# First norm of a two-layer decoder trunk: squares of x as the weights of one-column matmuls, and an inverse root in nine VectorE instructions

## The chip, the core and the metric

The kernel runs on one core of a Trainium2 chip. A core has TensorE (PE, with its weight loads listed apart as PEld), VectorE (DVE), ScalarE (ACT), GpSimdE (POOL) and SyncE (SP, which issues most DMAs). The metric is the device time of one execution in microseconds. All data are float32; most large products split their operands into a high and a low part and sum three products of parts.

## The reference

x has 512 tokens of 1024 channels, and c is one conditioning vector. Two layers follow each other, each with a token mixer (layer 0 a state-space mixer called S5, layer 1 an attention called FoX) and a gated feed-forward network with a short convolution (FFN). Ahead of each of the four sub-layers stands a norm by token, whose result is scaled and shifted by values computed from c; a last norm ends the kernel. This is the part that the change touches:

```python
def rmsnorm(x, g):
    x32 = x.astype(jnp.float32)
    y = x32 * lax.rsqrt(jnp.mean(x32 * x32, axis=-1, keepdims=True) + EPS)
    return (y * g.astype(jnp.float32)).astype(x.dtype)

def adaln_params(c, w, b):
    mod = jax.nn.silu(c) @ w + b
    shift, scale, gate = jnp.split(mod, 3, axis=-1)
    return shift[:, None, :], scale[:, None, :], gate[:, None, :]

def modulate(x, g, shift, scale):
    return rmsnorm(x, g) * (1.0 + scale) + shift

for i in range(DEPTH):                                  # DEPTH = 2
    shift, scale, gate = adaln_params(c, ada_w[i, 0], ada_b[i, 0])
    hn = modulate(h, norm_g[i, 0], shift, scale)
    m = s5_mixer(hn, ...) if i % 2 == 0 else fox_mixer(hn, ...)
    h = h + gate * m
    ...                                                 # the same with conv_ffn
return rmsnorm(h, final_g)
```

## The kernel before

The residual `h` lies in on-chip memory as eight tiles of 128 channels by 512 tokens (KT = 8, S = 512); a block of 128 tokens is one of NB = 4. So a sum over channels is a sum over partitions and over the eight tiles, and it is done by matmuls.

The work runs in stages, one after another: a prologue (the first norm and the start of S5), the S5 stage, FFN 0, FoX, FFN 1 and the last norm. In the prologue the order on PE, ACT, DVE and SP is the order in which the code is written (`manual_schedule`). Elsewhere a scheduler orders the instructions of each engine from the dependences and from costs that it assumes, so an edit in one place can move instructions of its neighbourhood. Each engine runs its own queue in order and waits for other engines by semaphores. A tile from a pool with n buffers can be written only when the tile n places earlier has been read for the last time.

The first norm, in `s5`, goes like this. SP issues four loads of `x`, then the loads of the first modulation's weights `ada_w`, 512 KB each, into `raw`, `w_hi` and `w_lo` buffers. ACT squares one tile of h after another into `nm_t` (L1113), a pool of two buffers. PE multiplies each square by a 128x128 matrix of ones (L1114): the sums over channels come out on all 128 partitions, with the 512 tokens along the row. ACT copies the sums (L1116), and PE turns the four blocks of 128 tokens around with transposes (L1119), so that each partition holds its own token's sum; column 0 of each block is the input of the inverse root.

The inverse root (`inv_root`, L391 to L401) starts from an integer trick and corrects twice, in eleven DVE instructions on a few columns, each of which needs the one before. In the prologue they are interleaved with the 25 instructions of `s5_turns` on `s_turn`, which need nothing of the norm. Behind them on DVE stands more parameter work of S5 (L701 to L881), then `ga` (L167), then the normed x, `a_x` (L1130).

On PE, behind the norm, stand 16 matmuls of the first modulation (`ada_pe`, L205, with the vector c as weights of 32 columns and `ada_w` as the moving operand, four of them side by side in the array), then `rms_rows` (L410), which spreads the inverse roots along rows, then the columns of the modulation (`ada_columns`, L157 and L162), whose result feeds `ga`. `a_x` needs `ga` and L410; the first product of S5 (L1144) needs `a_x`, and between its matmuls stand those of the second modulation (L205 again).

The later norms use `rms_stats` (L380): DVE has added up the squares of seven tiles (`ssq`), and this sum and the eighth square are the weights of matmuls whose moving operand is the column of ones `self.one`. They work on halves of 256 tokens, so nb is 2. Then come `inv_root`, `rms_rows`, and for each tile `nm_h` (L430, DVE), `a_hi` (L433, ACT) and `a_lo` (L434, DVE). The last norm (`norm_out`) scales the second half by the root in L469 and sends it out.

Of the kernel before, what the change touches and what calls it, by code (L numbers as in the profile page):

```python
# [8 lines left out]
F32 = mybir.dt.float32  # L9
F32R = mybir.dt.float32r  # L10
I32 = mybir.dt.int32
AF = mybir.ActivationFunctionType
ALU = mybir.AluOpType
# [4 lines left out]
P = 128  # L18
D = 1024
KT = D // P  # L20
S = 512
NB = S // P
# [36 lines left out]
def fill(pool, n):  # L59

    pool.tile([P, n // 4], F32, name="fill", bufs=1)
# [12 lines left out]
class Trunk:  # L74
# [311 lines left out]
    def inv_root(self, ps, nb, log=None):  # L386
        v, r, t, y = (self.small.tile([P, nb], I32 if n == "r" else F32, name=f"rs_{n}") for n in "vrty")
        e = self.nc.vector
        f = r.bitcast(F32)
        steps = (  # L390
            lambda: e.tensor_scalar(v, ps, 1.0 / D, EPS, op0=ALU.mult, op1=ALU.add),  # L391
            lambda: e.tensor_scalar(r, v.bitcast(I32), -0.5, float(0x5F3759DF), op0=ALU.mult, op1=ALU.add),
            lambda: e.tensor_tensor(t, f, f, ALU.mult),
            lambda: e.tensor_tensor(t, t, v, ALU.mult),
            lambda: e.scalar_tensor_tensor(t, t, -1.25 / 0.375, t, op0=ALU.add, op1=ALU.mult),
            lambda: e.tensor_scalar(t, t, 0.375, 1.875, op0=ALU.mult, op1=ALU.add),
            lambda: e.tensor_tensor(y, f, t, ALU.mult),
            lambda: e.tensor_tensor(t, y, y, ALU.mult),
            lambda: e.tensor_tensor(t, t, v, ALU.mult),
            lambda: e.tensor_scalar(t, t, -0.5, 1.5, op0=ALU.mult, op1=ALU.add),  # L400
            lambda: e.tensor_tensor(y, y, t, ALU.mult),  # L401
        )
        in_turn(steps) if log is None else log.extend(steps)
        return y
# [268 lines left out]
def in_turn(*logs):  # L673

    order = sorted(((n + 0.5) / len(l), i, n) for i, l in enumerate(logs) for n in range(len(l)))
    for _, i, n in order:
        logs[i][n]()
# [104 lines left out]
class S5(Trunk):  # L782
# [297 lines left out]
    def s5(self, i, nxt):  # L1080
        nc, tc = self.nc, self.tc
# [4 lines left out]
        with ExitStack() as stack:  # L1086
            spool = lambda name, st: st.enter_context(tc.tile_pool(name=name, bufs=1, reuse_waits="tile"))
            keep = spool("s5p", stack)
            self.first = self.load_pack("first", FIRST, keep)
            nc.scalar.activation(self.sc, self.first["c"], AF.Silu)  # L1090
            ones = keep.tile([P, P], F32, name="s5_ones")
            nc.vector.memset(ones, 1.0)
            self.s5q = spool("s5q", stack)
            with ExitStack() as start:
                tp = spool("s5t", start)
# [10 lines left out]
                with tc.manual_schedule(engines={ENG.PE, ENG.Activation, ENG.DVE, ENG.SP}):  # L1106
                    self.load_x(self.act)
                    self.load_rest()
                    self.s5_planes(keep)
                    ps = self.mm.tile([P, S], F32, name="mmp")  # L1110
                    for k in range(KT):
                        sq = self.tmp.tile([P, S], F32, name="nm_t")
                        nc.scalar.activation(sq, self.h[:, k, :], AF.Square)  # L1113
                        nc.tensor.matmul(ps, ones, sq, start=(k == 0), stop=(k == KT - 1))  # L1114
                    rows = self.tmp.tile([P, S], F32, name="nm_t")
                    nc.scalar.activation(rows, ps, AF.Copy)  # L1116
                    stats = self.aux.tile([P, NB, P], F32, name="aux")
                    for b in range(NB):
                        nc.tensor.transpose(stats[:, b], rows[:, b * P:(b + 1) * P], self.ident)  # L1119
                    params = self.s5_params(keep, tp, self.first["s5_prm"], stats[:, :, 0])  # L1120
                    y = next(params)
                    scale = self.ada_pe(i, (1,), late=True)
                    for _ in range(KT // 2):
# [11 lines left out]
                    ps = self.mm.tile([P, S], F32, name="mmp")  # L1135
# [71 lines left out]
            ps = self.aux.tile([KT, P], F32, name="aux")  # L1207
            nc.tensor.transpose(ps, self.sc, self.ident)
            rows = self.tmp.tile([KT, P], F32, name="nm_h", bufs=4)
# [61 lines left out]
        with tc.tile_pool(name="s5b", bufs=1, reuse_waits="tile") as pool:  # L1271
# [15 lines left out]
            after, y = nxt  # L1287
# [358 lines left out]
```

## Time and profile before

| | |
|---|---|
| time, median of 3 runs | 1217.13 us (1215.23 to 1223.22) |
| the profiled execution | 1217.02 us, its span from first to last instruction 1215.2 us |
| TensorE busy | 1180.3 us (97%), weight loads 1015.4 us (84%) |
| VectorE busy | 1007.6 us (83%) |
| ScalarE busy | 609.8 us (50%) |
| GpSimdE busy | 83.9 us (7%) |
| mean granted TensorE clock | 0.995 |
| moved by DMA | 183.81 MB, 151 GB/s on average |

All times in rows are microseconds from the first instruction. A row of the timeline holds start, duration, engine, line, operation, tiles as out<-in, shape, count, and in brackets the engine's idle time before it with what ended it. A row of the chain of waits holds start, duration, and what ran there. A row of the table by stretch holds the stretch, its length, then for PE, PEld, DVE, ACT and POOL the busy time and number of instructions, then the granted clock of PE (1.00 is full), the busy share of the DMA engines and the GB/s. A matmul of float32 operands appears as two records on PE, each with a weight load; most of the large products are one record. Ends of matmuls are modelled, so start-to-start distances tell more than durations.

### The profile page before, as it was taken

The numbers are of one execution on the slowest core, as the hardware profiler recorded it, in microseconds if no ns is written. First come the engines' busy times: TensorE is split into PE (matmuls) and PEld (weight loads), VectorE is DVE, ScalarE is ACT, GpSimd is POOL, SyncE is SP. The second block draws the span as 40 slices with busy tenths as digits, with TensorE's granted clock in tenths as the row PEclk, the third lists the DMA queues.
The fourth block names the chain that finished last, engine by engine and source line by source line (L and its number), as shares of the span: only waits on it lengthen the run. The fifth ranks groups of instructions, "written<-read, shape, count | busy, mean of one in ns | idle before, by whom it ended". The sixth has DMA issues, their size and how long they took to land.

```text
span 1215.2 us, 20334 instructions
## 1 busy us (share of the span) xinstructions
PE 1180.3 (97%) x7793; PEld 1015.4 (84%) x7793; DVE 1007.6 (83%) x1872; ACT 609.8 (50%) x1156; POOL 83.9 (7%) x145
## 2 busy tenths in 40 slices
PE   7999999999999999999999999999999999999997
PEld 2566688898989899889899777878989999999987
DVE  7999977789899988898687578875899887888965
ACT  3644555336445454455443565654466554555543
POOL 0000000100000000000000333430000000000000
PEclk9999999999999999999999999999999999999999
DMA  9778786622455544553445543432213332333331
GB/s 348 243 250 261 233 294 220 210 77 70 136 179 164 189 155 148 169 168 106 126 153 180 172 153 130 148 108 88 89 53 113 112 119 90 103 104 109 109 100 70
DMA packets 74512, 183.81 MB, mean 151 GB/s; under 512 B 23231, under 2 KB 25631, under 8 KB 73391
## 3 DMA queue, kind: packets, MB, share of 16 engines
q1 hardware_dynamic: 68367, 161.02, 40.5%
q0 software_dynamic: 5760, 20.97, 5.4%
q8 instruction: 61, 1.00, 0.3%
q10 hardware_dynamic: 288, 0.52, 0.1%
q14 instruction: 36, 0.29, 0.1%
HBM read 175.57 MB, written 6.92 MB: 150 GB/s over the span
## 4 chain that ended last, share of the span: by engine, by line
PE 56%; issue 26%; DVE 8%; DMA 5%; ACT 2%; POOL 2%; SPq 0%; POOLq 0%; DVEq 0%; ACTq 0%
PE mmp L294 24%; PE mmp L550 11%; PE aux L550 4%; PE mmp L1366 3%; PE mmp L1174 2%; DVE w_lo L278 2%; PE mmp L1203 2%; POOL ada_raw L233 1%; PE aux L1505 1%; DMA ada_raw<-in_ada_t 1%; PE aux L1065 1%; PE mmp L1114 1%; PE aux L1057 1%; PE aux L978 1%; DMA yt<-s_yd 1%
## 5 line engine op out<-in xcount | busy, mean ns | idle before, releaser
L278 DVE TENSOR_TENSOR w_lo<-raw,w_hi 128x1024 fp32r<-128x1024 f32 (+4 forms) x173 | 183.3, 1064 | 37.6 <-ACT w_hi L277 31.8
L277 ACT ACTIVATE w_hi<-raw 128x1024 fp32r<-128x1024 f32 (+4 forms) x173 | 154.8, 904 | 105.4 <-PE mmp L294 48.6
L294 PE MATMUL mmp<-ghi,w_hi 128*128 128x512 f32 (+1 forms) x392 | 145.5, 371 | 0.0
L294 PE MATMUL mmp<-ghi,w_lo 128*128 128x512 f32 (+1 forms) x392 | 144.7, 369 | 0.7 <-DVE w_lo L278 0.6
L294 PE MATMUL mmp<-glo,w_hi 128*128 128x512 f32 (+1 forms) x392 | 145.1, 370 | 0.0
L294 PE MATMUL mmp<-a_hi,w_hi 128*128 128x512 f32 (+1 forms) x376 | 138.4, 371 | 1.5 <-ACT a_hi L433 1.5
L294 PE MATMUL mmp<-a_hi,w_lo 128*128 128x512 f32 (+1 forms) x376 | 136.2, 363 | 0.2 <-DVE w_lo L278 0.2
L294 PE MATMUL mmp<-a_lo,w_hi 128*128 128x512 f32 (+1 forms) x376 | 135.7, 362 | 0.0
L550 PE MATMUL mmp<-w_hi 128*128 128x256 f32 x396 | 109.7, 277 | 2.7 <-ACT nm_h L557 2.3
L550 PE MATMUL mmp<-w_hi,w_lo 128*128 128x256 f32 x396 | 109.5, 277 | 0.7 <-DVE w_lo L278 0.7
L550 PE MATMUL mmp<-w_lo,w_hi 128*128 128x256 f32 x396 | 109.4, 276 | 0.0
L557 ACT ACTIVATE nm_h<-mmp 128x256 f32<-128x256 f32 x99 | 37.2, 381 | 107.3 <-PE mmp L550 107.3
L278 DVE TENSOR_TENSOR w_lo<-sums,w_hi 128x1024 fp32r<-128x1024 f32 x74 | 90.0, 1219 | 0.0
L277 ACT ACTIVATE w_hi<-sums 128x1024 fp32r<-128x1024 f32 x74 | 77.0, 1055 | 23.7 <-DVE sums L518 21.7
L294 PEld LDWEIGHTS mmp<-ghi,w_lo 128*128 128x128 f32 x392 | 74.7, 190 | 13.8 <-DVE w_lo L278 1.5
L294 PEld LDWEIGHTS mmp<-ghi,w_hi 128*128 128x128 f32 x392 | 74.7, 191 | 11.5 <-ACT w_hi L277 0.2
L294 PEld LDWEIGHTS mmp<-glo,w_hi 128*128 128x128 f32 x392 | 74.8, 191 | 11.1
L294 PEld LDWEIGHTS mmp<-a_hi,w_hi 128*128 128x128 f32 x376 | 70.2, 188 | 13.8 <-issue 2.6
L294 PEld LDWEIGHTS mmp<-a_hi,w_lo 128*128 128x128 f32 x376 | 70.6, 188 | 12.2 <-DVE w_lo L278 1.2
L294 PEld LDWEIGHTS mmp<-a_lo,w_hi 128*128 128x128 f32 x376 | 70.7, 188 | 9.7
L362 DVE SCALAR_TENSOR_TENSOR h<-mmp,par,h 128x512 f32<-128x512 f32 (+1 forms) x100 | 68.0, 681 | 12.1 <-PE mmp L294 11.9
L550 PEld LDWEIGHTS mmp<-w_hi 128*128 128x128 f32 x396 | 74.3, 188 | 3.2 <-ACT nm_h L557 2.5
(319 smaller groups left out, 3077.7 us busy)
## 6 DMA issues: line engine op xcount, KB each, us to landing
raw<-in_w_up SPq DMA_DIRECT2D x88, 512.0 KB, 3.3
raw<-in_ada_w SPq DMA_DIRECT2D x40, 512.0 KB, 5.6
ada_raw<-in_ada_t POOLq DMA_DIRECT2D x40, 512.0 KB, 3.9
nf<-nfd SPq DMA_DIRECT2D x8, 1152.0 KB, 6.5
raw<-in_fox_qk SPq DMA_DIRECT2D x16, 512.0 KB, 3.7
raw<-in_w_down SPq DMA_DIRECT2D x24, 320.0 KB, 3.1
rawd<-in_w_down SPq DMA_DIRECT2D x24, 256.0 KB, 3.3
raw<-in_w_down SPq DMA_DIRECT2D x16, 384.0 KB, 3.5
```

The source lines that it names most:

```text
L233: (nc.gpsimd if late else nc.sync).dma_start(ws[n], src)
L277: nc.scalar.activation(hi, src, AF.Copy)
L278: return nc.vector.tensor_tensor(lo, src, hi.bitcast(F32), ALU.subtract)
L294: self.last_mm = self.nc.tensor.matmul(o, wt, xt[:, cols], start=(k == 0 and n == 0), stop=(k == nk - 1 and n == 2),)
L362: add = self.nc.vector.scalar_tensor_tensor(self.h[:, m, cols], ps, self.par[i][:, 16 + m:17 + m], self.h[:, m, cols], op0=ALU.mult, op1=A ...
L550: self.last_mm = nc.tensor.matmul(o, wt[:, k], xt[:, k], start=(first and k == 0 and n == 0), stop=(k == H - 1 and n == 2), skip_group_che ...
L557: a = nc.scalar.activation(t, o, AF.Copy)
L978: nc.tensor.matmul(ps[:, :, cols], x[:, q, r].rearrange("p c j -> p (c j)"), both[:, :, planes, q, :], start=(r == 0), stop=(r == 1), skip ...
L1057: nc.tensor.matmul(yp[g2][:, k, :], t[:, g].rearrange("p c i -> p (c i)"), u[:, g, :], start=(k == 0), stop=False, skip_group_check=True,)
L1174: nc.tensor.matmul(ps, w[m][:, k, :], x[:, k], start=(k == 0), stop=(k == KT - 1))
L1203: nc.tensor.matmul(gps[m], wt, xt[:, k], start=(k == 0 and part == 0 and xt is yhi), stop=(k == KT - 1 and part == 1))
L1366: self.last_mm = nc.tensor.matmul(ps[q, b][:, :n], xt[:, k, tb], wt, start=(k == 0 and i == 0), stop=(k == KT - 1 and i == 2),)
```

## The change

Two edits. In the prologue the matrix of ones, the copy and the transposes go. Each block of 128 tokens of a square becomes the weights of a matmul whose moving operand is the column of ones, and the result, one number per token on that token's partition, is accumulated over the eight tiles. That is 4 matmuls for each of the eight squares, 32 in all. `fill(keep, 512)` keeps the room that the ones took, so that the other tiles stay where they were. In `inv_root`, used by all norms, a scale that was applied in an instruction of its own is carried into later constants: nine instructions in place of eleven.

```diff
         f = r.bitcast(F32)
+        a = 0.375
         steps = (
             lambda: e.tensor_scalar(v, ps, 1.0 / D, EPS, op0=ALU.mult, op1=ALU.add),
             lambda: e.tensor_scalar(r, v.bitcast(I32), -0.5, float(0x5F3759DF), op0=ALU.mult, op1=ALU.add),
             lambda: e.tensor_tensor(t, f, f, ALU.mult),
             lambda: e.tensor_tensor(t, t, v, ALU.mult),
-            lambda: e.scalar_tensor_tensor(t, t, -1.25 / 0.375, t, op0=ALU.add, op1=ALU.mult),
-            lambda: e.tensor_scalar(t, t, 0.375, 1.875, op0=ALU.mult, op1=ALU.add),
-            lambda: e.tensor_tensor(y, f, t, ALU.mult),
+            lambda: e.scalar_tensor_tensor(t, t, -1.25 / a, t, op0=ALU.add, op1=ALU.mult),
+            lambda: e.scalar_tensor_tensor(y, t, 1.875 / a, f, op0=ALU.add, op1=ALU.mult),
             lambda: e.tensor_tensor(t, y, y, ALU.mult),
-            lambda: e.tensor_tensor(t, t, v, ALU.mult),
-            lambda: e.tensor_scalar(t, t, -0.5, 1.5, op0=ALU.mult, op1=ALU.add),
-            lambda: e.tensor_tensor(y, y, t, ALU.mult),
+            lambda: e.scalar_tensor_tensor(t, t, -0.5 * a ** 3, v, op0=ALU.mult, op1=ALU.mult),
+            lambda: e.scalar_tensor_tensor(y, t, 1.5 * a, y, op0=ALU.add, op1=ALU.mult),
         )
...
-            ones = keep.tile([P, P], F32, name="s5_ones")
-            nc.vector.memset(ones, 1.0)
+            fill(keep, 512)
...
-                    ps = self.mm.tile([P, S], F32, name="mmp")
+                    stats = self.aux.tile([P, NB], F32, name="aux")
                     for k in range(KT):
                         sq = self.tmp.tile([P, S], F32, name="nm_t")
                         nc.scalar.activation(sq, self.h[:, k, :], AF.Square)
-                        nc.tensor.matmul(ps, ones, sq, start=(k == 0), stop=(k == KT - 1))
-                    rows = self.tmp.tile([P, S], F32, name="nm_t")
-                    nc.scalar.activation(rows, ps, AF.Copy)
-                    stats = self.aux.tile([P, NB, P], F32, name="aux")
-                    for b in range(NB):
-                        nc.tensor.transpose(stats[:, b], rows[:, b * P:(b + 1) * P], self.ident)
-                    params = self.s5_params(keep, tp, self.first["s5_prm"], stats[:, :, 0])
+                        for b in range(NB):
+                            nc.tensor.matmul(
+                                stats[:, b:b + 1], sq[:, b * P:(b + 1) * P], self.one,
+                                start=(k == 0 and b == 0), stop=(k == KT - 1), skip_group_check=True,
+                            )
+                    params = self.s5_params(keep, tp, self.first["s5_prm"], stats)
```

What stands first in PE's queue shows the first edit. Before (line numbers of the old file; `s_ones` is the matrix of ones, `rest` holds the identity):

```order
L1114 MATMUL mmp<-nm_t,s_ones 128x512 x8
L1119 MATMUL aux<-rest,nm_t 128x128 x4
L205 MATMUL mmp<-raw,s_sc_202 32x512 x16
L410 MATMUL aux<-rest,rs_y 128x128 x4
L157 MATMUL aux<-rest 128x8
```

And of the change (its lines count three fewer from here on; `one` is the column of ones):

```order
L1113 MATMUL aux<-one,nm_t 128x1 x32
L205 MATMUL mmp<-raw,s_sc_218 32x512 x16
L409 MATMUL aux<-rest,rs_y 128x128 x4
L157 MATMUL aux<-rest 128x8
L162 MATMUL aux<-sel,ada_rows 128x2 x4
```

The two groups at the head became one of 32, and what follows stands as before. The chain of the inverse root stands on DVE in the prologue, after the parameters of S5. Its end before:

```order
L399 TENSOR_TENSOR rs_t<-rs_t,rs_v 128x4
L908 SCALAR_TENSOR_TENSOR s_turn<-s_turn 128x32
L909 TENSOR_SCALAR s_turn<-s_turn 128x32
L907 SCALAR_TENSOR_TENSOR s_turn<-s_turn 128x32
L400 TENSOR_SCALAR rs_t<-rs_t 128x4
L908 SCALAR_TENSOR_TENSOR s_turn<-s_turn 128x32
L909 TENSOR_SCALAR s_turn<-s_turn 128x32
L401 TENSOR_TENSOR rs_y<-rs_y,rs_t 128x4
L913 TENSOR_SCALAR s_turn<-s_turn 128x6x32
```

And of the change:

```order
L399 SCALAR_TENSOR_TENSOR rs_t<-rs_t,rs_v 128x4
L906 SCALAR_TENSOR_TENSOR s_turn<-s_turn 128x32
L907 SCALAR_TENSOR_TENSOR s_turn<-s_turn 128x32
L908 TENSOR_SCALAR s_turn<-s_turn 128x32
L400 SCALAR_TENSOR_TENSOR rs_y<-rs_t,rs_y 128x4
L912 TENSOR_SCALAR s_turn<-s_turn 128x6x32
```

The root still ends just ahead of the last `s_turn` row, and two of its rows are gone. The last rows of DVE's queue are the root of the last norm's second half. Before:

```order
L391 TENSOR_SCALAR rs_v<-aux 128x2
L392 TENSOR_SCALAR rs_r<-rs_v 128x2
L393 TENSOR_TENSOR rs_t<-rs_r 128x2
L394 TENSOR_TENSOR rs_t<-rs_t,rs_v 128x2
L395 SCALAR_TENSOR_TENSOR rs_t<-rs_t 128x2
L396 TENSOR_SCALAR rs_t<-rs_t 128x2
L397 TENSOR_TENSOR rs_y<-rs_r,rs_t 128x2
L398 TENSOR_TENSOR rs_t<-rs_y 128x2
L399 TENSOR_TENSOR rs_t<-rs_t,rs_v 128x2
L400 TENSOR_SCALAR rs_t<-rs_t 128x2
L401 TENSOR_TENSOR rs_y<-rs_y,rs_t 128x2
L469 TENSOR_SCALAR o_tok<-aux,rs_y 128x512 x2
```

And of the change:

```order
L392 TENSOR_SCALAR rs_v<-aux 128x2
L393 TENSOR_SCALAR rs_r<-rs_v 128x2
L394 TENSOR_TENSOR rs_t<-rs_r 128x2
L395 TENSOR_TENSOR rs_t<-rs_t,rs_v 128x2
L396 SCALAR_TENSOR_TENSOR rs_t<-rs_t 128x2
L397 SCALAR_TENSOR_TENSOR rs_y<-rs_t,rs_r 128x2
L398 TENSOR_TENSOR rs_t<-rs_y 128x2
L399 SCALAR_TENSOR_TENSOR rs_t<-rs_t,rs_v 128x2
L400 SCALAR_TENSOR_TENSOR rs_y<-rs_t,rs_y 128x2
L468 TENSOR_SCALAR o_tok<-aux,rs_y 128x512 x2
```

Here nothing stands between the rows, and each needs the one before. At the other norms and at the start of both FFN stages the scheduler also exchanges neighbouring rows, on PE, DVE and ACT; GpSimd's and SP's queues are the same as before.

## The prediction

> **What bounds the kernel now.** I read the engine shares first, then the stages in a table by stretch, then the first 27 us instruction by instruction, since the larger edit stands there.
>
> ```profile
> PE 1180.3 (97%) x7793; PEld 1015.4 (84%) x7793; DVE 1007.6 (83%) x1872; ACT 609.8 (50%) x1156; POOL 83.9 (7%) x145
> ...
> 0.00:27.40 27.40, 18.45 (x78) 7.53 (x78) 20.39 (x145) 9.34 (x17) 2.66 (x22) 1.00 0.90 341
> 27.40:200.00 172.60, 171.29 (x1215) 115.01 (x1216) 154.45 (x239) 93.95 (x251) 1.28 (x2) 1.00 0.80 259
> ```
>
> TensorE (PE) is busy 97% of the span, and after 27.4 us it is nearly gapless (171.29 of 172.60 us). What delays that stream at its start delays the end. So the prologue is worth its full length, up to the first matmul on the normed x (L1144). These are its rows, from the timeline and the chain of waits:
>
> ```profile
> 5.54 1.15 ACT L1113 ACTIVATE nm_t<-h 128x512 f32<-128x512 f32 x2 [1.08 <-DMA h<-in_x]
> 8.33 0.63 ACT L1113 ACTIVATE nm_t<-h 128x512 f32<-128x512 f32 x1 [1.64 <-PE mmp L1114]
> 6.22 10.38 PE mmp L1114 x16
> 16.63 0.60 ACT L1116 ACTIVATE nm_t<-mmp 128x512 f32<-128x512 f32 x1 [1.22 <-PE mmp L1114]
> 17.28 0.65 PE aux L1119 x4
> 17.97 0.16 DVE L391 TENSOR_SCALAR rs_v<-aux 128x4 f32<-128x4 f32 x1 [3.12 <-PE aux L1119]
> 21.07 0.25 DVE L913 TENSOR_SCALAR s_turn<-s_turn 128x192 f32<-128x192 f32 x1
> 17.86 3.80 PE L205 MATMUL mmp<-raw,s_sc 128*32 128x512 f32 x32
> 21.60 1.16 PE L410 MATMUL aux<-rest,rs_y 128*128 128x128 f32 x8
> 22.73 1.03 PE L162 MATMUL aux<-sel,ada_rows 128*128 128x2 f32 x8
> 23.70 0.62 PE L205 MATMUL mmp<-raw,s_sc 128*32 128x512 f32 x2
> 26.44 0.16 DVE L167 SCALAR_TENSOR_TENSOR ga<-aux,rest 128x8 f32<-128x8 f32 x1
> 27.43 1.12 PE L1144 MATMUL mmp<-a_x,raw 128*128 128x512 f32 x2 [2.07 <-DVE a_x L1130]
> ```
>
> The squares on ScalarE (ACT) wait for PE, which needs 10.38 us for eight products with ones. A copy and four transposes follow. VectorE (DVE) stood idle 3.12 us before `rs_v`, then worked without a pause to `ga` at 26.44. The PE branch had its last word for `ga` at about 23.7 (L162), so DVE's queue set the start of L1144, with 2.7 us to spare on PE.
>
> The eight products did not all cost the same:
>
> ```profile
> 6.00:12.00 6.00, 5.78 (x7) 2.42 (x8) 5.62 (x44) 2.20 (x5) 0.00 (x0) 1.00 1.02 401
> 12.00:16.60 4.60, 4.59 (x10) 1.27 (x8) 2.72 (x23) 2.27 (x4) 0.00 (x0) 1.00 1.03 418
> ```
>
> Each f32 matmul is two records. Seven records touch the first 6 us and ten the next 4.6: about 0.85 us each, then about 0.43 to 0.5. The clock column says 1.00 there, but the durations say that PE began at half speed and doubled near 12 us. This doubling is the point on which I rest the forecast.
>
> **The change, part by part.**
>
> *Norm on PE (term A).* Gone are eight 128x512 products, the copy (L1116), four transposes (L1119) and a memset. New are 32 instructions with a 128x128 block of squares as weights and one moving column: 64 records, each with a full weight load. The kernel already has this shape, in the later norms (L380), once at half clock and once at full. First the table by stretch around the half-clock place, then the timeline:
>
> ```profile
> 599.34:602.76 3.42, 1.46 (x13) 1.26 (x12) 1.97 (x5) 1.17 (x3) 0.00 (x0) 1.00 0.00 0
> 602.76:606.17 3.41, 3.26 (x16) 3.26 (x16) 0.49 (x2) 2.68 (x4) 0.00 (x0) 0.50 0.01 2
> 606.17:609.58 3.41, 3.41 (x17) 3.41 (x18) 2.74 (x9) 0.42 (x1) 0.00 (x0) 0.50 0.08 11
> 609.58:613.00 3.42, 3.42 (x32) 3.42 (x32) 3.12 (x11) 0.48 (x2) 0.00 (x0) 1.00 0.84 274
> ...
> 602.91 1.01 PE L380 MATMUL aux<-one,ssq 128*128 128x1 f32 x4 [2.11 <-DVE ssq L356]
> 603.79 0.56 PE L294 MATMUL mmp<-ghi,w_hi 128*128 128x256 f32 x1
> 605.85 0.85 PE L380 MATMUL aux<-one,nm_t 128*128 128x1 f32 x4
> 606.56 0.56 PE L294 MATMUL mmp<-ghi,w_hi 128*128 128x256 f32 x1
> ...
> 1196.23 0.61 PE L380 MATMUL aux<-one,ssq 128*128 128x1 f32 x4
> 1196.70 0.36 PE L294 MATMUL mmp<-ghi,w_hi 128*128 128x256 f32 x1
> 39.42 1.95 PE L1155 MATMUL aux<-par,raw 128*128 128x1 f32 x16 [0.27 <-ACT par L170]
> 41.23 0.27 PE L1208 MATMUL aux<-rest,sc 128*8 128x128 f32 x1
> ```
>
> At half clock four records take 0.88 us (602.91 to 603.79) or 0.71 (605.85 to 606.56, the first weights loaded behind a wide matmul): 0.22 or 0.18 each. At full clock they take 0.47 / 4 = 0.12, and L1155's sixteen, 1.81 / 16 = 0.11. So a square costs 8 x 0.22 = 1.76 us at half clock and 0.94 at full, against about 1.7 and 0.9 for the wide product now. **The new form is no cheaper than the old one at the same clock.** What it saves for certain is the copy and the transposes, 16.60 to 17.93 = 1.33 us.
>
> Which clock will it have? In the stretch from 602.76 PE is busy 3.26 of 3.41 us, yet the clock stays at 0.50. Taking off the one-column records (0.88 and 0.32 us) leaves 2.06 us of wide streaming, 60%. The next stretch has 3.41 - 0.39 = 3.02 us of it, 88%, and the clock is full after it. I read this as: only streamed columns count, and the release wants more than 60% and at most 88% of a stretch of 3.41 us. The new norm streams one column per record, so I take it to stay at half clock throughout: 64 x 0.22 = 14.1, end at 6.22 + 14.1 = 20.3 (17.6 at 0.18), where today the statistics are ready at 17.93. ACT needs only some 0.6 us per square (5.54 to 6.69 for two) and isn't the limit.
>
> The Trainium skill, "TensorE: Matmul & The Clock Gate", section on the HAM clock gate, says that the array starts at 1.2 GHz and goes to 2.4 after about 3.4 us of sustained activity; the halving agrees with the rows above (0.85 to 0.43), but it doesn't say whether weight loads count as activity. By its rule taken plainly the release would come as it does now, near 12 us, and the sum would be that of the first rival.
>
> *What follows in the prologue.* DVE starts `rs_v` at 20.3 in place of 17.97: +2.3. The chain of inverse root and `s_turn`, 34 instructions from 17.97 to 21.07, is 0.09 each, so two fewer give -0.2: DVE is ready for `ga` at 26.44 + 2.1 = 28.6. PE runs L205 next (32 records, 17.86 to 21.60, 3.7 us at full clock). These stream 512 columns each, so I let them release the clock after one and a half stretches, 5.1 us: that does 2.55 us' worth, the other 1.15 follow, end at 26.6. L410 to L162 take 21.60 to 23.76 = 2.2, so `ga` can go at 28.8. **A = +2.3**; from -0.5 (0.18 per record, DVE then first) to +3.5 (L205 at half clock to the end: 20.3 + 7.4 + 2.2 = 29.9).
>
> The weight transfers move with it: raw buffers are freed by L205, so SP's next loads go later. In the table by stretch this hole is seen:
>
> ```profile
> 18.00:19.00 1.00, 1.00 (x12) 0.28 (x11) 1.00 (x12) 0.00 (x0) 0.00 (x0) 1.00 0.96 393
> 19.00:20.00 1.00, 1.00 (x12) 0.26 (x8) 1.00 (x13) 0.00 (x0) 0.00 (x0) 1.00 0.33 107
> 20.00:21.00 1.00, 1.00 (x14) 0.38 (x8) 1.00 (x13) 0.00 (x0) 0.00 (x0) 1.00 0.68 123
> ```
>
> The eight loads of the first modulation fill the queue to about 19.5. The hole ends when L205 has freed its first buffers; L205 starts 2.4 us later and its first quarter takes 0.9 us more at half clock, so the hole grows by 3.3. What is behind it is needed when L1144 starts, which is 2.3 us later itself. I add nothing; the upper end is the difference, +1.0.
>
> *The nine-instruction root in the later norms (term B).* The waits of PE that end on this chain:
>
> ```profile
> PE mmp L294 <- ACT a_hi L433: 1.5, 2, 0.8
> PE aux L410 <- DVE rs_y L401: 0.5, 2, 0.3
> ```
>
> Two steps of 0.20 us (next fence) are gone from each half. The two waits of 0.25 at L410 vanish (-0.5). Of the two of 0.76 at L433 I count 0.25 each, since DVE interleaves other work there. **B = -1.0**, from 0 to -2.0 (all of both rows).
>
> *The last norm (term C).* The kernel's end hangs on the second half's root, in the chain of waits:
>
> ```profile
> 1206.82 0.17 DVE rs_v L391
> ...
> 1208.80 0.17 DVE rs_y L401
> ...
> 1209.07 0.75 DVE o_tok L469
> ```
>
> Ten steps in 1.98 us; nothing runs beside them, so two fewer are **C = -0.4**.
>
> *Rows that only change places (term D).* The order also shifts neighbours in the norms and at the start of each FFN, where DVE is nearly full:
>
> ```profile
> L278 DVE TENSOR_TENSOR w_lo<-raw,w_hi 128x1024 fp32r<-128x1024 f32 (+4 forms) x173 | 183.3, 1064 | 37.6 <-ACT w_hi L277 31.8
> ...
> 262.00:300.00 38.00, 36.47 (x52) 1.00 0.21 70
> ```
>
> I value it at 0. From below it could close a 0.76 us gap of PE twice (-1.5), from above make PE wait for one more DVE operation of 1.06 us (the mean of L278) twice (+2.1).
>
> **The sum** against the profiled execution's own 1217.02 us (span 1215.2; 0.1 below the median, so no correction): +2.3 - 1.0 - 0.4 = +0.9, that is **1217.9 us**.
>
> **The rivals.** *(1) The clock is released as today.* If weight loads count, 6.0 us at 0.22 make 27 records to 12.25, and the other 37 x 0.12 = 4.4 end at 16.6. `rs_v` comes 1.3 earlier, with the shorter chain -1.5, and PE's 23.7 stays below the new 24.9. 1217.0 - 1.5 - 1.4 = 1214.1. For it: the page's plain wording, and a stretch at 95% busy might simply have missed a higher bar. Against: 602.76 to 606.17. Chance 0.25.
>
> *(2) It does all that its words say.* If a record costs 0.12 whatever the clock, the norm ends at 6.22 + 7.7 = 13.9, below DVE's own 14.85 (17.97 less its idle 3.12). `ga` then waits for L162 at 23.75, since the loads still fill the queue to about 19.5 and the last of L205 waits for them: -2.7. 1217.0 - 2.7 - 1.4 = 1212.9. The same page, section on LDWEIGHTS, gives columns / 1.2 ns for a load (107 ns for 128), without naming a clock; the trace agrees at full clock (0.11 to 0.12) and differs at half (0.22), and the measurement decides. Chance 0.10.
>
> *(3) Slower.* L205 uses 32 of 128 array columns per matmul. If the monitor weighs that, the clock stays half through L205, L410 and L162: 20.3 + 7.4 + 4.4 = 32.1 for `ga`, +5.7, and L1144 with its L205 neighbours spends another stretch or two of 3.41 us at half clock, which puts off +1.7 to 3.4. Together +8.2, 1217.0 + 8.2 - 1.4 = 1223.8. It decides if L205 alone doesn't lift the clock before L410. Four L205 groups run side by side, which speaks against it. Chance 0.12.
>
> **How the numbers follow.** The forecast has 0.53. A half-clock stretch like that at 602.76 costs 6.83 / 2 = 3.4 us and depends on where a gap falls, so single runs scatter (1215.2 to 1223.2 before); the range takes that in with the bounds of A to D and reaches over rivals 1 and 2 and to rival 3: 1212 to 1223.5. A difference under 1% (12 us) is what a measurement of this kernel can't tell from no change, and all cases lie inside it: within 1% 0.95, faster 0.02, slower 0.03 (rival 3 with another half-clock stretch).
>
> **What the new profile would show.** For the forecast: 64 one-column records on PE from 6.2 to about 20, squares on ACT that start about 1.7 us apart to the last, `rs_v` after 18.5, a first full-clock stretch that begins only in L205, `ga` past 27.5. Rival 1 shows the squares' spacing halving near 12 us and `rs_v` near 16.6; rival 2 squares 0.6 to 1.0 us apart and DVE without idle before `rs_v`; rival 3 L1144 records of 0.85 us. For B and C: no wait of L410 on `rs_y`, and eight steps of 0.20 before `o_tok`. The forecast is wrong if records of one column cost under 0.15 at half clock, or if the stream after 27 us has slack that swallows the shift.

## The result, and the profile after

| | before | changed |
|---|---|---|
| median | 1215.17 us (21 runs) | 1219.48 us (21 runs) |
| ratio, 95% interval | | 1.0025 [1.0014, 1.0035], that is +3.0 us (1.7 to 4.3) |
| the profiled execution | 1217.02 us | 1219.48 us (span 1217.6) |

The change made the kernel slightly slower. One execution of each kernel (of before and of the changed one, about 200 and 250 us slower than the rest) is left out of the ratio; of the other 20 the means lie 3.1 us apart and the medians 3.9. The forecast was 1217.9 us (range 1212 to 1223.5) and "within 1%". The size of the difference was missed: +0.9 forecast, +3.0 measured. That the time itself came closer is partly luck, since the profiled execution of before, on which the sum was made, lies 1.9 us above the median of its 21 runs.

Line numbers are three lower than before: the squares are L1111, the norm's matmuls L1113, the inverse root L392 to L400, `rms_rows` L409, `a_x` L1127, the first product of S5 L1141, the one-column sums L1152 (L1155 before, the name that the expectations below use). Every experiment shifts its lines by a few more, so rows are best matched by their tiles. First the timeline of the changed kernel's prologue:

```profile
5.37 1.15 ACT L1111 ACTIVATE nm_t<-h 128x512 f32<-128x512 f32 x2 [0.89 <-DMA h<-in_x]
6.05 13.81 PE L1113 MATMUL aux<-one,nm_t 128*128 128x1 f32 x64 [6.05 <-ACT nm_t L1111]
8.01 0.63 ACT L1111 ACTIVATE nm_t<-h 128x512 f32<-128x512 f32 x1 [1.49 <-PE aux L1113]
9.72 0.63 ACT L1111 ACTIVATE nm_t<-h 128x512 f32<-128x512 f32 x1 [1.08 <-PE aux L1113]
...
16.55 0.63 ACT L1111 ACTIVATE nm_t<-h 128x512 f32<-128x512 f32 x1 [1.09 <-PE aux L1113]
19.79 5.99 PE L205 MATMUL mmp<-raw,s_sc 128*32 128x512 f32 x32
19.90 0.16 DVE L392 TENSOR_SCALAR rs_v<-aux 128x4 f32<-128x4 f32 x1 [5.04 <-PE aux L1113]
...
28.35 0.16 DVE L167 SCALAR_TENSOR_TENSOR ga<-aux,rest 128x8 f32<-128x8 f32 x1
29.35 1.98 PE L1141 MATMUL mmp<-a_x,raw 128*128 128x512 f32 x4 [0.47 <-DVE a_x L1127]
```

ACT starts a square every 1.71 us from 8.01 to 16.55 without ever speeding up, because PE takes 13.81 us for 64 records, 0.216 each. DVE now stands idle 5.04 us before `rs_v` (3.12 before). `ga` comes 1.91 us later than before and L1141 1.92. The table by stretch shows where the clock rises:

```profile
8.87:12.29 3.42, 3.42 (x18) 3.42 (x18) 3.25 (x28) 1.26 (x2) 0.00 (x0) 1.00 1.04 419
12.29:15.70 3.41, 3.41 (x18) 3.41 (x18) 2.43 (x20) 1.26 (x2) 0.00 (x0) 1.00 1.03 418
...
23.00:24.00 1.00, 1.00 (x8) 0.19 (x4) 0.93 (x8) 0.00 (x0) 0.00 (x0) 1.00 0.61 156
24.00:25.00 1.00, 1.00 (x12) 0.31 (x8) 0.90 (x7) 0.00 (x0) 0.00 (x0) 1.00 0.98 377
```

The clock column reads 1.00 throughout and is no help before the first recorded change; the counts are. PE was busy to the last hundredth from 8.87 to 15.70, yet only 18 records touch each stretch. L205's records go from 8 to 12 per microsecond within 24 to 25, and in the trace's clock records the first full-clock stretch starts at 24.58. Before, it started at 12.25.

In the wait list of PE the two rows on the root that the prediction quotes are gone (two rows that are there are shown), and the chain of waits at the end is shorter:

```profile
PE mmp L549 <- ACT nm_h L556: 6.0, 4, 2.7
...
PE mmp L205 <- DMA raw<-in_ada_w: 0.4, 1, 0.4
```

```profile
1209.62 0.17 DVE rs_v L392
...
1211.20 0.17 DVE rs_y L400
...
1211.47 0.75 DVE o_tok L468
```

From `rs_v` to the last `rs_y` it is 1.58 us, against 1.98 before.

### The profile page after: what moved, and what is told of

It reads as the page before. It is cut to its first block, busy times and chain, and to the rows that moved or that the text cites. A ratio compares the mean times of both kernels' runs of the same rounds, so it can differ in the third digit from the quotient of the medians.

```text
span 1217.6 us, 20405 instructions
## 1 busy us (share of the span) xinstructions
PE 1185.9 (97%) x7837; PEld 1026.0 (84%) x7837; DVE 1006.6 (83%) x1853; ACT 608.9 (50%) x1155; POOL 83.7 (7%) x145
## 5 line engine op out<-in xcount | busy, mean ns | idle before, releaser
L294 PE MATMUL mmp<-ghi,w_hi 128*128 128x512 f32 (+1 forms) x392 | 145.9, 372 | 0.0
L294 PE MATMUL mmp<-ghi,w_lo 128*128 128x512 f32 (+1 forms) x392 | 145.0, 370 | 0.8 <-DVE w_lo L278 0.6
L294 PE MATMUL mmp<-glo,w_hi 128*128 128x512 f32 (+1 forms) x392 | 145.2, 371 | 0.0
L294 PE MATMUL mmp<-a_hi,w_hi 128*128 128x512 f32 (+1 forms) x376 | 137.8, 369 | 0.0
L294 PE MATMUL mmp<-a_hi,w_lo 128*128 128x512 f32 (+1 forms) x376 | 136.0, 362 | 0.3 <-DVE w_lo L278 0.3
L294 PE MATMUL mmp<-a_lo,w_hi 128*128 128x512 f32 (+1 forms) x376 | 135.7, 362 | 0.0
L549 PE MATMUL mmp<-w_hi 128*128 128x256 f32 x396 | 110.0, 278 | 4.8 <-ACT nm_h L556 4.3
L549 PE MATMUL mmp<-w_hi,w_lo 128*128 128x256 f32 x396 | 109.5, 277 | 1.1 <-DVE w_lo L278 1.1
L549 PE MATMUL mmp<-w_lo,w_hi 128*128 128x256 f32 x396 | 109.5, 276 | 0.0
L294 PEld LDWEIGHTS mmp<-ghi,w_lo 128*128 128x128 f32 x392 | 74.8, 191 | 14.1 <-DVE w_lo L278 1.8
L294 PEld LDWEIGHTS mmp<-ghi,w_hi 128*128 128x128 f32 x392 | 74.9, 191 | 11.7 <-ACT w_hi L277 0.4
L294 PEld LDWEIGHTS mmp<-glo,w_hi 128*128 128x128 f32 x392 | 74.9, 191 | 11.0
L294 PEld LDWEIGHTS mmp<-a_hi,w_lo 128*128 128x128 f32 x376 | 70.6, 188 | 11.9 <-DVE w_lo L278 0.7
L294 PEld LDWEIGHTS mmp<-a_hi,w_hi 128*128 128x128 f32 x376 | 70.2, 188 | 12.0 <-issue 2.6
L549 PEld LDWEIGHTS mmp<-w_hi 128*128 128x128 f32 x396 | 74.3, 188 | 5.8 <-ACT nm_h L556 5.1
L294 PEld LDWEIGHTS mmp<-a_lo,w_hi 128*128 128x128 f32 x376 | 70.7, 188 | 9.5
```

The costliest lines, as they stand in the source:

```text
L294: self.last_mm = self.nc.tensor.matmul(o, wt, xt[:, cols], start=(k == 0 and n == 0), stop=(k == nk - 1 and n == 2),)
L549: self.last_mm = nc.tensor.matmul(o, wt[:, k], xt[:, k], start=(first and k == 0 and n == 0), stop=(k == H - 1 and n == 2), skip_group_che ...
```

## The experiments

Each kernel was timed 12 times, beside 35 runs of the kernel before on the same chip. Ratios are against before, with 95% intervals, and the difference in us is worked out from the ratio with 1214 us. All differences are small: most intervals are 3 to 5 us wide, so two experiments that lie 2 us apart can't be told from each other.

| experiment | ratio | us |
|---|---|---|
| norm edit alone | 1.0042 [1.0026, 1.0058] | +5.1 (3.2 to 7.0) |
| root edit alone | 0.9986 [0.9971, 1.0000] | -1.7 (-3.5 to 0) |
| changed, with wide products ahead | 0.9999 [0.9979, 1.0019] | -0.1 |
| old norm, wide products ahead, new root | 0.9977 [0.9963, 0.9992] | -2.8 (-4.5 to -1.0) |
| changed, 128 columns per record | 0.9998 [0.9982, 1.0014] | -0.2 |
| the same, wide products ahead | 0.9995 [0.9981, 1.0010] | -0.6 |
| the same, and L1152 with 128 columns | 0.9998 [0.9979, 1.0017] | -0.2 |
| changed, once more | 1.0034 [1.0020, 1.0048] | +4.1 (2.4 to 5.8) |
| root alone, L1152 with 128 columns | 0.9982 [0.9967, 0.9997] | -2.2 |
| old norm, wide products, new root, L1152 with 128 columns | 0.9985 [0.9967, 1.0002] | -1.8 |
| changed, two loads earlier | 1.0030 [1.0013, 1.0047] | +3.6 (1.6 to 5.7) |
| old norm, wide products, new root, L1152 with 128, two loads earlier | 0.9980 [0.9966, 0.9994] | -2.4 |

**The two edits apart.** The norm alone keeps the eleven-instruction root:

```diff
-        a = 0.375
-            lambda: e.scalar_tensor_tensor(t, t, -1.25 / a, t, op0=ALU.add, op1=ALU.mult),
-            lambda: e.scalar_tensor_tensor(y, t, 1.875 / a, f, op0=ALU.add, op1=ALU.mult),
+            lambda: e.scalar_tensor_tensor(t, t, -1.25 / 0.375, t, op0=ALU.add, op1=ALU.mult),
+            lambda: e.tensor_scalar(t, t, 0.375, 1.875, op0=ALU.mult, op1=ALU.add),
+            lambda: e.tensor_tensor(y, f, t, ALU.mult),
...
```

> The first edit alone (one-column matmuls in the first norm, the old eleven-instruction root). Outside the prologue every engine's order is that of the kernel before. Theory (the one-column stream keeps the TensorE clock at half): +2 to +3.5 us against the kernel before, rs_v near 19.9, ga about 2 us later than before, clock released only in L205. Rival (the loss sits in the rows that changed places in later stages): 0 within 1 us against the kernel before.

The root alone has the other half of the diff, in the kernel before.

> The second edit alone (nine-instruction root, the old first norm with the matrix of ones). Outside the prologue every engine's order is that of the changed kernel. Theory: -1 to -2 us against the kernel before: two steps of 0.20 us less at the end, and the waits of PE at L410 on the root gone. Rival (the new order costs): +1 to +4 us, with PE waits in FFN 0 that the kernel before does not have.

The norm alone costs +5.1 us, the root alone gives -1.7; their sum, +3.4, is what the changed kernel shows (+3.0 and, run once more, +4.1). So the whole loss is the norm's. In the timeline of the norm alone:

```profile
5.81 13.81 PE L1114 MATMUL aux<-one,nm_t 128*128 128x1 f32 x64 [5.81 <-ACT nm_t L1112]
...
29.11 1.98 PE L1142 MATMUL mmp<-a_x,raw 128*128 128x512 f32 x4 [1.19 <-DVE a_x L1128]
```

The same 13.81 us, and its first full-clock stretch starts at 22.9. The prologue explains 1.7 of the 5.1 us (29.11 against 27.43); 2 to 3.5 us were expected.

Where does the rest arise? A later mark is the first statistics of the next norm (L380), behind the S5 stage. The root alone has the same order outside the prologue as the changed kernel, so their rows can be set side by side. The root alone, the changed kernel, the changed kernel run once more, and before:

```profile
26.85 1.98 PE L1143 MATMUL mmp<-a_x,raw 128*128 128x512 f32 x4 [1.73 <-DVE a_x L1129]
245.37 0.50 PE L380 MATMUL aux<-one,ssq 128*128 128x1 f32 x4
```

```profile
250.11 0.50 PE L380 MATMUL aux<-one,ssq 128*128 128x1 f32 x4
```

```profile
28.88 1.98 PE L1141 MATMUL mmp<-a_x,raw 128*128 128x512 f32 x4 [0.51 <-DVE a_x L1127]
249.53 0.50 PE L380 MATMUL aux<-one,ssq 128*128 128x1 f32 x4
```

```profile
247.23 0.50 PE L380 MATMUL aux<-one,ssq 128*128 128x1 f32 x4
```

Against the root alone the changed kernel is 2.50 us late at the first product and 4.74 at L380; run once more, 2.03 and 4.16. Against before it is only 2.88 and 2.30 late at L380, since PE waits there on `kt` (0.48 us at 70.13) and on `ua` (0.43 at 160.21), which the root alone doesn't. The norm alone is 2.99 behind before at L380 (250.22), of which 1.54 are a lost stretch of clock that is told below. So by 250 us something between nothing and 2 us has come on top of the prologue's delay, and single executions don't say more.

**Do only streamed columns count?** Ahead of the changed norm stand four 128x512 products of ones that nobody reads (extra work):

```diff
+                    lift = self.mm.tile([P, S], F32, name="mmp")
+                    for k in range(4):
+                        nc.tensor.matmul(lift, ones, ones[:, None, :].to_broadcast([P, NB, P]), start=True, stop=True)
```

> The changed kernel, with four 128x512 products of a matrix of ones ahead of the norm on PE (from about 1 us, 6.8 us of work at half clock), whose result nobody reads. Theory (only streamed columns count): the clock is released between 4.5 and 8 us and taken back one or two stretches of 3.41 us later although PE is busy with one-column matmuls all the time; rs_v between 14.9 and 18.5; 1 to 3 us faster than the changed kernel. Rival (weight loads hold a clock that is once released): no half clock after the release, the norm at 0.94 us per square, rs_v at 14.9 to 15.5, 3 us or more faster than the changed kernel.

The timeline (from 2.1 us on; the first of the eight wide records starts at 1.09) and the table by stretch of this kernel:

```profile
2.10 4.84 PE L1108 MATMUL mmp<-s_ones 128*128 128x512 f32 x7
6.78 8.84 PE L1117 MATMUL aux<-one,nm_t 128*128 128x1 f32 x64
15.55 5.83 PE L205 MATMUL mmp<-raw,s_sc 128*32 128x512 f32 x32
```

```profile
5.46:8.87 3.41, 3.41 (x24) 2.66 (x22) 3.13 (x23) 1.35 (x4) 0.00 (x0) 1.00 0.98 359
8.87:12.29 3.42, 3.42 (x33) 3.42 (x32) 3.25 (x29) 2.37 (x4) 0.00 (x0) 1.00 1.03 421
12.29:15.70 3.41, 3.41 (x20) 3.39 (x24) 2.46 (x21) 0.63 (x1) 0.00 (x0) 0.50 1.03 416
15.70:19.12 3.42, 3.42 (x20) 0.79 (x20) 3.42 (x36) 0.00 (x0) 0.00 (x0) 0.50 1.06 416
19.12:22.53 3.41, 3.41 (x31) 1.63 (x23) 3.06 (x20) 0.60 (x1) 0.00 (x0) 1.00 1.00 351
```

The wide products release the clock at 5.46. The stretch from 8.87 holds nothing on PE but one-column records, 33 at full speed, with PE and its weight loads busy all of 3.42 us, and the clock is **taken back** at 12.29. The next release, at 19.12, follows a stretch that L205 fills. In time this kernel equals before and is some 3 to 4 us faster than the changed kernel (0.9999 against 1.0025 and 1.0034), where 1 to 3 were expected; `rs_v` starts at 15.66.

The counter-test leaves the number of records and the weight loads alone and gives each record 128 equal columns to stream:

```diff
-                    stats = self.aux.tile([P, NB], F32, name="aux")
+                    stats = self.aux.tile([P, NB, P], F32, name="aux")
...
-                                stats[:, b:b + 1], sq[:, b * P:(b + 1) * P], self.one,
+                                stats[:, b], sq[:, b * P:(b + 1) * P], ones,
...
-                    params = self.s5_params(keep, tp, self.first["s5_prm"], stats)
+                    params = self.s5_params(keep, tp, self.first["s5_prm"], stats[:, :, 0])
```

> The changed kernel with one thing other: the moving operand of the 32 matmuls is the matrix of ones, 128 columns in place of one. The same 64 records and the same weight loads, but each streams 128 columns. Theory (streamed columns decide the clock, and a record is as long as its weight load): the clock is released between 9.6 and 13 us, the norm ends near 16.6, rs_v between 15.5 and 17.2, ga near 24.9; 3 to 6 us faster than the changed kernel, 2 to 4 faster than the kernel before. Rival (many small records with weight loads are slow as such, whatever they stream): the norm ends near 20 as in the changed kernel, and the time is that of the changed kernel.

Its timeline and its table by stretch:

```profile
5.92 9.69 PE L1114 MATMUL aux<-s_ones,nm_t 128*128 128x128 f32 x64 [5.92 <-ACT nm_t L1112]
...
24.58 0.17 DVE L167 SCALAR_TENSOR_TENSOR ga<-aux,rest 128x8 f32<-128x8 f32 x1 [0.34 <-PE aux L162]
```

```profile
8.87:12.29 3.42, 3.42 (x26) 3.35 (x26) 3.25 (x29) 1.72 (x3) 0.00 (x0) 1.00 1.04 420
12.29:15.70 3.41, 3.41 (x33) 3.23 (x35) 2.48 (x21) 1.43 (x3) 0.00 (x0) 1.00 1.03 418
```

With 128 times the columns the norm takes 9.69 us in place of 13.81: the clock comes at 10.09, and a record costs no more: 33 of them touch a full-clock stretch, as with one column, and the weight loads are busy for 3.23 of its 3.41 us. On the clock the theory holds. Against the changed kernel on the same chip it is some 4 us faster (ratios 0.9998 and 1.0034; 3 to 6 were expected), so the loss goes when the clock is there: that it comes from the half clock in the norm is shown. Against before the time was missed: 2 to 4 us faster was expected, and it equals before, though `ga` comes 1.86 us earlier than there.

Wide products ahead of this norm bring the release to 5.62 and `ga` to 24.25:

> The kernel with 128 moving columns, and the four unread wide products ahead of the norm. Theory: the clock is released between 4.5 and 8 us and, unlike with one column, not taken back at the end of one or two stretches; norm at full clock from there, rs_v at 14.7 to 15.6; ga near 24, since the loads of the first modulation set L205; 0 to 1.5 us faster than without the four products. Rival: the clock is taken back before 20 us, rs_v past 15.6, as with one column.

The released clock is held until 39.75. The time can't be told from that without the products (0.9995 and 0.9998).

And the old norm with the same four products, and the new root:

> The old first norm with wide products, the nine-instruction root, and the four unread products ahead of the norm. Theory: the wide products keep the released clock, 0.86 us per square, statistics ready by 15.5, DVE without idle before rs_v or under 0.6 us of it, ga near 24; 2 to 3 us faster than the root alone, 3.5 to 4.5 us faster than the kernel before. Rival (the stream after 27 us has slack that swallows a shift of the prologue): the same as the root alone.

This kernel gains 2.8 us on before, where 3.5 to 4.5 were expected; the interval reaches the expectation, but the gain is not to be told from the root's own 1.7 either. DVE still stood idle 0.91 us before `rs_v`, and `ga` came at 24.57. The changed kernel was timed once more beside the kernels with 128 columns:

> The changed kernel once more, on the same chip as the three above. Theory: the first full-clock stretch begins in L205, after 21 us, whatever the phase of the stretches; rs_v at 19.3 to 20.3; 2 to 5 us slower than the kernel before.

All of it came: the release at 24.05, `rs_v` at 19.41, and +4.1 us.

**A second place where the clock is lost.** In five of these traces a half-clock stretch of 3.41 us stood near 40 us. There PE has little to stream: L157, L162, then L1152 (16 one-column records). I gave L1152 128 equal columns as well:

```diff
-                    col = self.aux.tile([P, 1], F32, name="aux")
+                    col = self.aux.tile([P, P], F32, name="aux")
...
-                            col, w[0][:, k, :], self.par[i][:, k:k + 1], start=(k == 0), stop=(k == KT - 1)
+                            col, w[0][:, k, :], self.par[i][:, k:k + 1].to_broadcast([P, P]), start=(k == 0), stop=(k == KT - 1)
...
-                    nc.scalar.activation(shifted, col, AF.Copy)
+                    nc.scalar.activation(shifted, col[:, 0:1], AF.Copy)
```

> As the kernel with 128 columns and the four products ahead, and the sixteen one-column records of L1155 (near 39 us) stream 128 equal columns too. Theory: no half-clock stretch begins between 36 and 50 us, where three of the four profiles of the first experiments with the changed norm or with the products ahead show one of 3.41 us; 0 to 1.5 us faster than without this edit. Rival (such stretches there cost nothing, since PE waits for ACT and DVE between 40 and 70 us): the same time.

The table by stretch without this edit, and then with it:

```profile
36.20:39.60 3.40, 3.13 (x26) 2.84 (x26) 3.23 (x11) 1.95 (x7) 0.00 (x0) 1.00 0.01 2
39.60:43.01 3.41, 3.41 (x6) 1.31 (x5) 3.38 (x6) 3.41 (x7) 0.00 (x0) 0.52 0.59 192
```

```profile
36.20:39.60 3.40, 3.13 (x25) 2.79 (x25) 3.23 (x9) 1.85 (x6) 0.00 (x0) 1.00 0.05 17
39.60:43.01 3.41, 3.41 (x9) 1.43 (x8) 3.34 (x7) 3.41 (x7) 0.00 (x0) 1.00 0.54 177
```

The clock stays, and the 16 products behind it (L1175, 39.17) take 7.12 in place of 8.73 us. Over the 12 runs each the mean granted clock rises from 0.9932 to 0.9950, some 4.5 us less at half clock. In the total nothing of it can be told (0.9998 and 0.9995). The rows say why: this edit also changes the scheduler's order in the S5 stage, and PE now waits there for DVE and ACT:

```profile
160.24 2.00 PE L1064 MATMUL aux<-ua,w 64*128 64x63 f32 x32 [0.47 <-DVE ua L1046]
...
174.05 1.20 PE L1204 MATMUL mmp<-a_hi,w_hi 128*128 128x512 f32 x4 [1.28 <-ACT a_hi L1192]
```

At its first L1204 this kernel is 1.47 us ahead of the one without the edit (154.93 and 156.40), at its first L294 1.10 behind (185.50 and 184.40). All four kernels with this edit wait 1.28 us at that place, and no other does. So the exchanged rows cost some 2.5 us, as much as the clock can have gained, and the times of this edit don't price the clock. The same edit with the root alone, and with the old norm:

> The old first norm, the nine-instruction root, and the sixteen records of L1155 with 128 equal columns (the scheduler then also exchanges some neighbouring rows in the S5 stage). Theory (a half-clock stretch near 40 us costs about 1 us, and only in part of the executions): 0 to 1 us faster than the root alone, no half clock between 36 and 50 us. Rival (the exchanged rows matter more): slower than the root alone.

> The old first norm behind the four unread products, the nine-instruction root, and L1155 with 128 columns: all that the runs so far point to. Theory: clock at full from 4.5 to 8 us on and none of it lost before 300 us; ga near 24.5; 3 to 5 us faster than the kernel before. Rival (the transfers of the second modulation set the pace behind ga, so that a prologue earlier than before brings nothing): as the root alone, 1 to 2 us faster than the kernel before.

Both lie with the root alone (0.9986). For the second 3 to 5 us below before were expected and 1.8 came, what its rival said; the exchanged rows stand in it too. In none of the four kernels with 128 columns in L1152 is there a half-clock stretch near 40 us.

The traces say why this stretch comes and goes. From the first release on, the clock changes on a grid of 3.413 us. In the norm alone that grid has a point at 22.9 + 6 x 3.413 = 43.38:

```profile
40.11 0.28 PE L157 MATMUL aux<-rest 128*128 128x8 f32 x2
40.25 1.03 PE L162 MATMUL aux<-sel,ada_rows 128*128 128x2 f32 x8
41.55 1.95 PE L1153 MATMUL aux<-par,raw 128*128 128x1 f32 x16 [0.27 <-ACT par L170]
...
43.52 8.66 PE L1172 MATMUL mmp<-a_x,raw 128*128 128x512 f32 x16
```

The narrow patch lasts from 40.11 to 43.52, as long as a stretch, and fills the stretch of the grid from 39.97 to 43.38 nearly whole: 0.14 of 3.41 us, 4%, are left for wide matmuls. In the next stretch the clock is half, and L1172 takes 8.66 in place of 7.12 us, **+1.54**. The same sum for the weakest stretch of each execution without the edit, with the share of it that lies outside the narrow patch as the streaming share:

| kernel | release, a point of the grid | weakest stretch | streaming share | clock after it |
|---|---|---|---|---|
| changed, wide products ahead | 19.12 | 36.19 to 39.60 | 0.02 | half |
| norm alone | 22.90 | 39.97 to 43.38 | 0.04 | half |
| old norm, wide products, new root | 5.85 | 36.57 to 39.98 | 0.11 | half |
| 128 columns, wide products ahead | 5.62 | 36.34 to 39.75 | 0.16 | half |
| 128 columns | 10.09 | 37.40 to 40.81 | 0.31 | half |
| two loads earlier | 24.77 | 38.42 to 41.83 | 0.33 | half |
| changed | 24.58 | 41.64 to 45.06 | 0.39 | full |
| changed, once more | 24.05 | 41.11 to 44.53 | 0.46 | full |
| before | 12.25 | 39.55 to 42.97 | 0.48 | full |
| root alone | 11.78 | 35.67 to 39.08 | 0.51 | full |

Six lost at up to 0.33, four kept from 0.39: the narrow patch costs a stretch only where the grid does not cut it in the middle. This rule was read from the traces afterwards. Its test is the edit of L1152: counted as narrow, the patch would have left 0.05 to 0.16 in three of the four kernels with 128 columns there, and all four kept the clock.

What places the grid isn't shown. The release lies on it, but in the six kernels with the unread products PE begins the same work at 1.09, and the release falls anywhere from 3.92 to 5.85. So whether this stretch is lost looks like an accident of the execution rather than a price of the edit. The granted clock of all timed runs bears this out (it counts only the time behind the first release). In the 35 runs of before beside the norm alone, the time follows the time at half clock (correlation 0.92, about 0.5 us for each us). But the norm alone has no more of it than before: its mean clock is 0.9951 against 0.9939, some 12 against 15 us at half clock. The lost stretches explain the scatter, not the +5.1 us.

**The transfers' hole.** The prediction gave it nothing. Two loads of the second modulation are issued without waiting for L205 here; the order on the engines is as in the changed kernel:

```diff
-        n = 0
+        n = int(i == 0 and thirds == (0,))
```

> The changed kernel with one thing other: the loads of the second modulation's weights begin with a pool that has free buffers, so that two of them (512 KB each) are issued without waiting for L205; the order on every engine is that of the changed kernel. Theory (the hole in the transfers, longer by the late L205, costs beyond ga): the first product on the normed x starts as in the changed kernel (29.0 to 29.5), but the later loads land 1.5 to 2.5 us earlier and PE is at the first state product (aux<-ua) by 72.5 in place of 74; 1 to 2 us faster than the changed kernel. Rival (DVE and ACT alone set the pace behind ga): the time of the changed kernel.

Rows of the timeline: of before, of the changed kernel, and of this one.

```profile
29.34 1.06 PE L205 MATMUL mmp<-raw,s_sc 128*32 128x512 f32 x8
...
59.60 1.92 PE L205 MATMUL mmp<-raw,s_sc 128*32 128x512 f32 x16
61.45 1.15 PE L1015 MATMUL aux<-u,w 128*64 128x64 f32 x32
...
70.87 2.00 PE L1065 MATMUL aux<-ua,w 64*128 64x63 f32 x32
```

```profile
31.26 1.52 PE L205 MATMUL mmp<-raw,s_sc 128*32 128x512 f32 x8
...
61.97 1.91 PE L205 MATMUL mmp<-raw,s_sc 128*32 128x512 f32 x12
64.32 1.05 PE L205 MATMUL mmp<-raw,s_sc 128*32 128x512 f32 x4 [0.44 <-DMA raw<-in_ada_w]
65.30 1.15 PE L1014 MATMUL aux<-u,w 128*64 128x64 f32 x32
...
73.98 1.22 PE L1064 MATMUL aux<-ua,w 64*128 64x63 f32 x18
```

```profile
30.92 1.06 PE L205 MATMUL mmp<-raw,s_sc 128*32 128x512 f32 x8
...
64.42 1.92 PE L205 MATMUL mmp<-raw,s_sc 128*32 128x512 f32 x16
66.28 1.15 PE L1014 MATMUL aux<-u,w 128*64 128x64 f32 x32
```

In the changed kernel L205 is held up twice: 1.52 in place of 1.06 us at 31, and 3.33 us from 61.97 to 65.30 where before took 1.85. With the earlier loads both are gone, but the time is that of the changed kernel (1.0030; this execution stood at half clock for 6.83 us from 41.83 instead). The 1 to 2 us that were expected did not show, and L1064 on `ua` starts at 74.95, where 72.5 was expected, since the half clock took some 3.3 us. Set beside the root alone, this execution is 2.15 us late at L1141 and 5.43 at L380, so without those 3.3 it would still be about 2 us late there, and not over 4 as the changed kernel. In the rows the early loads take away what arises behind the prologue; in the time (+3.6, 1.6 to 5.7) this isn't seen. What the hole is worth stays open. The last run puts this edit beside the earlier lifts:

> The kernel with the old norm, the four products ahead, the nine-instruction root and 128 columns in L1155, with the two early loads besides. Theory of the transfers: since L205 starts near 15.7 there and no hole is left, the early loads bring under 0.7 us; within 1 us of the same kernel without them. Rival (SP's queue behind L205 still costs): 1 to 2 us faster.

Its release is at 3.92 and `ga` at 23.45, 3.0 us ahead of before, and it comes out at 0.9980, within 1 us of the same kernel without the early loads, as the theory had it, and within the interval of the root alone. Three kernels beat before with an interval wholly below 1 (0.9977, 0.9980, 0.9982). All of them have the old norm and the new root, and none is to be told from the root by itself.

## Why the prediction was right or wrong

**The clock in the norm: right, and shown.** A record of 0.22 us (0.216 measured), `rs_v` at 20.3 (19.90), squares about 1.7 us apart to the last (1.71), release only in L205 (24.58, and 22.9 in the norm alone). Rival 1, a release as before, falls: it would have had `rs_v` near 16.6. Rival 2 falls with the record's length. Rival 3, half clock through L205, falls with the release at 24.58, about 4.8 us into L205. The rule on which the forecast rested was taken from a half-clock place at 602.76; the take-back at 12.29 and the 128 columns now carry it.

The Trainium skill, "TensorE: Matmul & The Clock Gate", section on the HAM clock gate, speaks of 3.4 us of sustained activity. The grid of 3.41 us agrees. Taken plainly it would have been met by these 13.8 us of matmuls; the runs say that a one-column matmul counts for next to nothing.

**The way to `ga`: right within 0.4 us.** Forecast 28.8, measured 28.35; +2.3 at L1144, measured +1.92 (+1.68 in the norm alone). PE was through L205 at 25.71 (26.6 in the sum; 0.5 of this is the earlier start), and DVE, ready at 28.35, not PE, spoke the last word.

**Term A as a whole: the step that failed.** It took the delay at L1144 for the edit's whole price, +2.3 with 3.5 as its upper end. The delay was right and the price was not: the norm alone measured +5.1 (3.2 to 7.0). "I add nothing" for what lies behind L1144 is the step that was wrong. In the profiled execution L205 waits behind late loads, +0.46 at 31 us and +1.48 at 62 to 65, which with the +1.92 makes +3.85 at L1014; 0.74 comes back by the first product on `ua` (73.98, before 70.87). The changed kernel run once more had +1.45 and +0.17 there, and against the root alone still 4.16 us at L380. With the early loads no such growth is left in the rows, which points at the late transfers, but no time confirms it. Lost stretches of clock are not the reason, since the norm alone has no more of them on average than before. So the price is measured and comes with the half clock in the norm; the way that 2 to 3 us of it take behind L1144 stays open.

**Terms B, C and D: right, as far as the runs tell.** C was -0.4 and the chain shows 1.58 against 1.98. The waits of L410 and L433 on the root are gone (2.0 us in all, of which B counted 1.0); the wait of L549 on `nm_h` reads 6.0 in place of 4.3 us (5.0 when the kernel was run once more, 4.5 with the root alone), for which I have no cause. Together -1.4 was forecast and the root alone measured -1.7 (-3.5 to 0), with the rows in their new places, so nothing speaks against D at 0, within that interval.

**The base.** One profiled execution, 1.9 us above the later median, was taken as the kernel. It isn't slow for want of clock (0.995, where the later runs have 0.994 on average); why it is slow isn't known. In these traces half-clock stretches stand at different places from one execution to the next (40 to 43, 353, 523 to 529, 599 to 608, 850 us). The prediction named that scatter and gave it to the range, which was right.

## What to carry to other kernels

Moving a reduction into the weights saves little by itself where the weight load is as long as the stream that it replaces (here 1.71 us per square at half clock in the new form, about 1.7 in the old). Narrow matmuls that filled most of a stretch of 3.41 us took TensorE's clock away here, or held it back, with PE at 100% busy. Read a PE stretch by its records per microsecond and its streamed columns, not by its busy share; where a narrow form is wanted, try it with 128 equal columns, and see what the scheduler then exchanges. A shift that the prologue gains or loses need not arrive unchanged: follow it down the timeline at two or three later marks, against a kernel with the same order, before giving it a price. And before a lost stretch in one trace is taken for a cause, compare the mean clock of all runs.

## What the runs showed of the hardware that I had not expected

- The clock is taken back with PE fully busy: one stretch of 3.41 us with only one-column records did it (12.29), and near 40 us stretches with up to 0.33 of their length outside the narrow patch did (six of six), while 0.39 and more kept it (four of four).
- L205, whose matmuls use 32 columns of the array each, four side by side, releases the clock: one stretch full of it was enough in the norm alone (L205 from 19.55, full clock at 22.9).
- Ahead of the first recorded change the clock column reads 1.00 although records take twice as long.
- 128 columns in place of one cost a record next to nothing: in the norm 33 records touch 3.41 us in both forms at full clock, and the sixteen of L1152 take 1.89 in place of 1.81 us (start to start).
- The clock changes on a grid of 3.413 us, and where the grid lies differs between executions that begin alike (release at 3.92 to 5.85 behind the same products).
